# Head sums in an RWKV7 mixer: from float32 products to pairs of float32r products, with two prefetch windows moved

## The chip, the cores and the metric

The kernel is one launch on 1 core of a Trainium2 chip. The metric is the time of that launch on the device in microseconds; the median of several runs is quoted, and every row shown comes from one further run that was profiled.

## The reference, cut to what matters

A diffusion transformer of four layers runs over 256 latent and 256 context tokens with 1024 features. Layers 0 and 3 mix tokens by grouped attention, layer 1 by neighbourhood attention, and layer 2 by a bidirectional RWKV7 recurrence; each is followed by a squared-ReLU MLP. The change touches layer 2 alone. There are 16 heads of 64 features, and the sums over a head's 64 features are these:

```python
kk = (k * p['k_k']).reshape(hs)
kk = kk * lax.rsqrt(jnp.maximum(jnp.sum(kk * kk, -1, keepdims=True), 1e-12))
...
mu = jnp.mean(y, -1, keepdims=True)
var = jnp.mean(jnp.square(y - mu), -1, keepdims=True)
y = (y - mu) * lax.rsqrt(var + RW_GN_EPS) * lnx_g + lnx_b
bonus = jnp.sum(jnp.sum(r[None] * k_dir * p['r_k'], -1, keepdims=True), axis=0) * v
y = (y + bonus).reshape(g.shape)
return (y * g) @ p['wo']
```

`y` is the sum of a forward and a backward scan with the state update `s = s*w + (s a) b + v k`. Between these sums lie the projections r, k, v (1024 x 1024 each), three low-rank gates and the scan.

## The kernel before

**Engines.** PE multiplies, ACT casts, copies and evaluates functions, DVE does tensor arithmetic, POOL solves small triangular systems, and SP issues all the DMAs named here.

**Weight products.** A large product is made of float32r products. `split` (L423 to L425) turns a float32 tile into a high part, a cast on ACT, and a low part, a subtraction on DVE; weights are split alike at L280 after their load into `wr`. `mm3` (L430 to L432) then issues three products for each block of 128 features: high by high, high by low, low by high. The projections r and k go through `gemm` (tile `mm`), v through `values` (tile `vps`, L479 to L481).

**The mixer.** `rwkv` works on pairs of heads: pair c holds 128 rows (two heads of 64) and 512 columns (tokens, in 8 blocks of 64), so there are 8 pairs. A sum over a head's 64 rows is a product with `ones64`, a 128 x 128 matrix with two blocks of ones, in plain float32. For each pair there are four lists of steps:

- `prep(c)`, 13 steps: the gates (`gate_products`: products into `wps`, then functions on ACT into `sg` and `ag`), `unit_k` (Square into `ksq`, head sum `kss` at L1192, then Ln and Exp), decays by a scan, `triangles` (product `tps`, masked by DVE into `TT`, the backward one transposed into `dc`, stored to DRAM as `dr`), and `solve` (DMA `dr` into `lane`, POOL solves, DMA to `rr`, DMA into `S`).
- `inverses(c)`, 10 steps: DVE transposes `S` into `R` (L1313), the products `pa`, `pb`, `pv`, `px` and the copies `Xt<-M` and `Xt<-px` put together the inverse of each 64 x 64 triangle.
- `core(c)`: the scan over 8 blocks in two directions; for each block products `nps`, `zps`, copy `z`, product `ups`, copy `u`, then `yps` and the state `sps`.
- `post(c)`, 6 steps: `mean` (copy `y` out of PSUM, sum `gm`, centring on DVE at L1486, Square into `ysq`), `bonus` (sum `bo`, transposed v into `vT`), `var` (sum `gv`, Ln, Exp), `normed`, `gated` (product `g` of 128 x 128 by 128 x 512) and `parts` (the split of `o`, the operand of the last projection).

**What sets the order.** Every step carries a due time counted in pairs; all steps are sorted by it and written out in that order, so each engine works through one fixed list. `over(steps, a, b)` spreads steps evenly from a to b:

```python
todo = over([keys(c) for c in range(8)], -2.6, -1.5)
todo += over([values(j, t) for j in range(4) for t in TOKS], -1.35, .3)
for c in range(8):
    main = core(c)
    todo += [(c + x / len(main), f) for x, f in enumerate(main)]
    todo += over(inverses(c), c - .65, c - .1)
    todo += over(post(c), c + 1, c + 1.6) if c < 7 else []
```

So prep runs one and a half to two and a half pairs ahead, and the stretch ahead of the first core, here called the transition, holds the key projections, the prep of pairs 0 and 1, and the value projections. The last `post` is woven with the beginning of the output projection (`mm<-o`). Tiles come from pools: `ps_s` gives the PSUM banks of the head sums, `tmp` and `pair` those in SBUF.

Of the kernel before, what the change touches and what calls it, by code (L numbers as in the profile page):

```python
# [10 lines left out]
F32 = mybir.dt.float32  # L11
F32R = mybir.dt.float32r
# [181 lines left out]
def dit_kernel(ctx: ExitStack, tc: tile.TileContext, places, t_in, out, layers=DEPTH):  # L194
# [767 lines left out]
    def rwkv(i, hx, gate, nrm, begun, ends):  # L962
# [36 lines left out]


        xx = [pair("xx") for _ in range(4)]

# [159 lines left out]
        def prep(c):  # L1162
# [24 lines left out]

            def unit_k():
                sq = tmp(512, "ksq")
                act.activation(out=sq, in_=k_, func=AF.Square, scale=C("k_k", "rw")[:, c:c + 1])  # L1190
                ps = bank(ps_s, 512, "kss")
                pe.matmul(ps, lhsT=ones64, rhs=sq, start=True, stop=True)  # L1192
                dve.tensor_scalar(out=sq, in0=ps, scalar1=1e-12, scalar2=None, op0=ALU.max)
                log(out=sq, in_=sq, func=AF.Ln)
                log(out=sq, in_=sq, func=AF.Exp, scale=-0.5)
                q["nkk"] = tmp(512, "nkk")
                dve.scalar_tensor_tensor(out=q["nkk"], in0=k_, scalar=nkk_c[:, c:c + 1], in1=sq, op0=ALU.mult, op1=ALU.mult)
# [279 lines left out]
        def post(c):  # L1477
            q = st[c]
            hold = {}

            def mean():
                y = tmp(512, "y")
                act.copy(out=y, in_=q["y"])
                ps = bank(ps_s, 512, "gm")
                pe.matmul(ps, lhsT=ones64, rhs=y, start=True, stop=True)
                dve.scalar_tensor_tensor(out=y, in0=ps, scalar=-1.0 / 64, in1=y, op0=ALU.mult, op1=ALU.add)  # L1486
                sq = tmp(512, "ysq")
                act.activation(out=sq, in_=y, func=AF.Square)
                hold["y"], hold["sq"] = y, sq

            def bonus():
                ps = bank(ps_s, 512, "bo")
                pe.matmul(ps, lhsT=ones64, rhs=q["rkd"], start=True, stop=True)
                bo = q["rkd"]
                act.copy(out=bo, in_=ps)
                pt = bank(ps_s, 512, "vT")
# [3 lines left out]
                dve.tensor_tensor(out=bo, in0=pt, in1=bo, op=ALU.mult)  # L1500
                hold["bo"] = bo

            def var():
                ps = bank(ps_s, 512, "gv")
                pe.matmul(ps, lhsT=ones64, rhs=hold["sq"], start=True, stop=True)
                r = hold["sq"]
                log(out=r, in_=ps, func=AF.Ln, bias=epg, scale=1.0 / 64)
                log(out=r, in_=r, func=AF.Exp, scale=-0.5)
# [6 lines left out]
            def gated():  # L1515
                ps = bank(ps_s, 512, "g")
                g2 = sml.tile([128, 128], F32, tag="g2", bufs=1, name="g2")
                sp.dma_start(out=g2, in_=t_in["rws"][c, :, 2])
                pe.matmul(ps, lhsT=g2, rhs=sig, start=True, stop=True)
                y = hold["y"]  # L1520
                dve.tensor_tensor(out=y, in0=y, in1=hold["bo"], op=ALU.add)
                dve.tensor_tensor(out=y, in0=y, in1=ps, op=ALU.mult)

            def parts():
                o[c] = pair("o", F32R)
                split(o[c], hold["y"], 0, 512)
            return [mean, bonus, var, normed, gated, parts]

# [34 lines left out]
        for c in range(8):  # L1563
            main = core(c)
            todo += [(c + x / len(main), f) for x, f in enumerate(main)]
            todo += over(inverses(c), c - .65, c - .1)
            todo += over(post(c), c + 1, c + 1.6) if c < 7 else []
            if c >= RHELD:
                todo.append((c - 2.9, lambda c=c: fetch(c)))
        for c in range(8):  # L1570
# [3 lines left out]
            def step(k, c=c, made_=made_):  # L1574
# [4 lines left out]
                return go  # L1579
            todo += over([step(k) for k in range(9)], c - 2.4, c - 1.5)  # L1580
            todo += over([step(k) for k in range(9, 13)], c - 1.4, c - .9)
        todo.append((7., last_weights))
# [216 lines left out]
```

## Time and profile before

| | us |
|---|---|
| median of 3 runs | 2552.61 |
| lowest and highest | 2551.04, 2557.27 |
| the profiled execution | 2547.62 |
| its span, first to last instruction | 2545.2 |
| PE busy in the span | 2448.7 (96%) |
| DVE busy | 1664.0 (65%) |
| ACT busy | 1188.7 (47%) |
| POOL busy | 209.2 (8%) |
| mean granted clock of PE | 0.987 |

The mixer's stretch lies between about 1240 and 1830 us of the span: gates, keys and values up to about 1440, the eight pairs from there to about 1800, and then the last `post`. A group's row names a line of the kernel, an engine, an operation and its tiles; its numbers are the busy time of the group, the mean of one in ns and, behind the bar, the idle time of the engine ahead of it. A float32 product of 128 x 512 leaves two records in the trace, so sixteen records are eight products.

### The profile page before, as it was taken

What the parts mean: (1) busy time and instruction counts of PE and PEld (TensorE: products, weight loads), DVE (VectorE), ACT (ScalarE), POOL (GpSimd) and SP (SyncE); (2) the same over time, 40 slices, a digit from 0 to 9 for tenths busy, and PEclk for the clock granted to TensorE, in tenths of its full rate; (3) what the DMA queues carried; (4) which work ended last, traced back from release to release, by engine and by line L of the source; (5) the groups of instructions that cost most, each with busy time, mean ns of one, the idle gap of its engine ahead of it and who ended that gap; (6) DMA issues with size and microseconds to landing.
All of it is one profiled execution on the core that took longest, in us unless ns stands there. A gap on an engine that the chain in (4) does not pass through costs nothing. (4 is left out here: it accounts for less than half of the span.)

```text
span 2545.2 us, 53184 instructions
## 1 busy us (share of the span) xinstructions
PE 2448.7 (96%) x22337; PEld 2085.8 (82%) x22337; DVE 1664.0 (65%) x3087; ACT 1188.7 (47%) x2226; POOL 209.2 (8%) x383
## 2 busy tenths in 40 slices
PE   8999999999999999999889799899999999998998
PEld 5779888889766988888867677778898888998997
DVE  4567777775566777787786565673567663766555
ACT  3555443244566543334555444544362343465644
POOL 0002000002000110000202112211020000121000
PEclk9999999999999999999999999999999999999999
DMA  8432556642211245665132311210336654223553
GB/s 337 166 127 75 182 189 192 207 157 88 69 55 58 88 152 182 207 205 176 60 112 77 80 28 33 41 20 15 143 107 216 206 184 126 93 68 115 175 184 98
DMA packets 158415, 324.11 MB, mean 127 GB/s; under 512 B 77393, under 2 KB 80993, under 8 KB 158177
## 3 DMA queue, kind: packets, MB, share of 16 engines
q1 hardware_dynamic: 158176, 320.73, 39.8%
q8 instruction: 175, 2.87, 0.5%
q14 instruction: 64, 0.52, 0.1%
HBM read 310.71 MB, written 9.97 MB: 126 GB/s over the span
## 5 line engine op out<-in xcount | busy, mean ns | idle before, releaser
L430 PE MATMUL mm<-h,wh 128*128 128x512 f32 (+1 forms) x1472 | 515.5, 351 | 6.1 <-ACT h L180 4.7
L432 PE MATMUL mm<-h,wl 128*128 128x512 f32 (+1 forms) x1472 | 511.6, 348 | 1.1 <-DVE wl L280 1.1
L280 DVE TENSOR_TENSOR wl<-wr,wh 128x1024 fp32r<-128x1024 f32 x363 | 442.7, 1227 | 103.5 <-ACT wh L180 77.9
L431 PE MATMUL mm<-h,wh 128*128 128x512 f32 (+1 forms) x1472 | 510.0, 347 | 0.3 <-DVE h L425 0.2
L180 ACT CAST wh<-wr 128x1024 fp32r<-128x1024 f32 x363 | 373.8, 1049 | 261.7 <-DVE wl L280 89.2
L430 PE MATMUL mm<-f,wh 128*128 128x512 f32 (+1 forms) x1168 | 397.6, 340 | 0.0
L432 PE MATMUL mm<-f,wl 128*128 128x512 f32 (+1 forms) x1168 | 397.6, 340 | 0.0
L431 PE MATMUL mm<-f,wh 128*128 128x512 f32 (+1 forms) x1168 | 397.0, 340 | 0.0
L430 PEld LDWEIGHTS mm<-h,wh 128*128 128x128 f32 x1472 | 279.4, 190 | 50.0 <-issue 8.8
L432 PEld LDWEIGHTS mm<-h,wl 128*128 128x128 f32 x1472 | 279.8, 190 | 37.1 <-issue 3.0
L431 PEld LDWEIGHTS mm<-h,wh 128*128 128x128 f32 x1472 | 279.8, 190 | 34.5 <-issue 2.8
L431 PEld LDWEIGHTS mm<-f,wh 128*128 128x128 f32 x1168 | 221.6, 190 | 24.7
L430 PEld LDWEIGHTS mm<-f,wh 128*128 128x128 f32 x1168 | 221.6, 190 | 24.5
L432 PEld LDWEIGHTS mm<-f,wl 128*128 128x128 f32 x1168 | 221.6, 190 | 24.2
L180 ACT ACTIVATE relu<-mm 128x512 f32<-128x512 f32 (+1 forms) x146 | 72.5, 497 | 360.4 <-PE mm L432 360.3
L425 DVE TENSOR_TENSOR f<-sqr,f 128x512 fp32r<-128x512 f32 (+1 forms) x146 | 82.4, 567 | 210.4 <-ACT f L180 210.4
L492 DVE SCALAR_TENSOR_TENSOR x<-mm,gate,x 128x256 f32<-128x256 f32 x280 | 127.3, 480 | 128.5 <-PE mm L432 128.3
L544 POOL TENSOR_SCALAR x<-zc,cs 128x256 f32<-128x256 f32 x88 | 86.0, 990 | 1302.9 <-DVE zc L575 1302.9
L387 DVE SCALAR_TENSOR_TENSOR mwt<-mwt,srow 128x1024 f32<-128x1024 f32 x144 | 175.8, 1221 | 8.3 <-DMA mwt<-in_mwr_dram 6.9
L387 DVE SCALAR_TENSOR_TENSOR mpr<-mwt,srow 128x1024 f32<-128x1024 f32 x112 | 136.7, 1220 | 0.5
L430 PE MATMUL mm<-o,wh 128*128 128x256 f32 (+1 forms) x400 | 120.1, 302 | 0.3 <-ACT o L180 0.2
L432 PE MATMUL mm<-o,wl 128*128 128x256 f32 (+1 forms) x400 | 119.9, 300 | 0.1
(292 smaller groups left out, 4317.9 us busy)
## 6 DMA issues: line engine op xcount, KB each, us to landing
wr<-in_gw_dram SPq DMA_DIRECT2D x363, 512.0 KB, 3.7
mwt<-in_mwr_dram SPq DMA_DIRECT2D x144, 512.0 KB, 4.3
mwt<-in_mw_dram SPq DMA_DIRECT2D x48, 512.0 KB, 5.4
srow<-srow_d SPq DMA_DIRECT2D x6, 512.0 KB, 4.1
nab<-in_nab_dram SPq DMA_DIRECT2D x8, 384.0 KB, 3.3
rk<-rk_d SPq DMA_DIRECT2D x6, 512.0 KB, 5.1
rk_d<-rkp SPq DMA_DIRECT2D x10, 256.0 KB, 2.2
x<-in_xt_dram SPq DMA_DIRECT2D x4, 512.0 KB, 10.2
```

The costliest lines, as they stand in the source:

```text
L180: x = f(*args, **kw)
L280: self.lo[self.done % len(self.lo)].tensor_tensor(out=lo, in0=t, in1=hi.bitcast(F32), op=ALU.subtract)
L387: dve.scalar_tensor_tensor(out=to, in0=t, scalar=1.0, in1=rw_["s"][cnd], op0=ALU.mult, op1=ALU.mult, accum_out=m[:, cnd, r * 8 + c:r * 8 + ...
L425: eng.tensor_tensor(out=dst[:, 1, a:b], in0=src, in1=dst[:, 0, a:b].bitcast(F32), op=ALU.subtract)
L430: pe.matmul(ps, lhsT=st, rhs=hl[:, 0, a:b], start=first, stop=False)
L431: pe.matmul(ps, lhsT=st, rhs=hl[:, 1, a:b], start=False, stop=False)
L432: pe.matmul(ps, lhsT=wl[:, c * 128:(c + 1) * 128], rhs=hl[:, 0, a:b], start=False, stop=last)
L492: dve.scalar_tensor_tensor(out=xc(c)[:, a:b], in0=ps[:, a - base:b - base], scalar=gate[:, cnd, c:c + 1], in1=xc(c)[:, a:b], op0=ALU.mult, ...
L544: (eng or dve).tensor_scalar(out=dst, in0=src, scalar1=ca, scalar2=cb, op0=ALU.mult, op1=ALU.add)
```

## The change

It has three parts, all in `rwkv`.

1. The four float32 head sums of a pair become two float32r products each. `in_parts` casts the operand to a high part on ACT and subtracts on DVE for the low part; `over_heads` multiplies both by `sums64`, the float32r copy of `ones64`. For the mean, the matrix is `less64` (identity minus `ones64`/64), so that `gm` comes out centred and the centring on DVE goes. y is no longer copied before `gm`; its parts are cast from PSUM, and the centred y is copied from `gm`. `unit_k` is cut in two steps, so `prep` has 14; `post` has 8. The product `g` moves from `gated` to `var`, the load of its weights to `bonus`.
2. `inverses(c)` goes in two groups: six steps from c - .74 to c - .42, four from c - .28 to c - .06.
3. The first ten steps of pair 0's `prep` go from -2.55 to -1.9 (nine from -2.4 to -1.5 before); those of other pairs keep their window.

```diff
@@ -998,6 +998,21 @@
         dve.tensor_scalar(out=ka1, in0=C("k_a", "rw"), scalar1=-1.0, scalar2=1.0, op0=ALU.mult, op1=ALU.add)
 
 
+        sums64 = sml.tile([128, 128], F32R, tag="sums64", bufs=1, name="sums64")
+        act.copy(out=sums64, in_=ones64)
+        less64 = sml.tile([128, 128], F32R, tag="less64", bufs=1, name="less64")
+        dve.scalar_tensor_tensor(out=less64, in0=ones64, scalar=-1.0 / 64, in1=ident, op0=ALU.mult, op1=ALU.add)
+
+        def in_parts(src):
+            t = pair("ip", F32R)
+            split(t, src, 0, 512)
+            return t
+
+        def over_heads(ps, w, parts):
+            for x in (1, 0):
+                pe.matmul(ps, lhsT=w, rhs=parts[:, x], start=x == 1, stop=x == 0)
+
+
         xx = [pair("xx") for _ in range(4)]
 
 
@@ -1185,11 +1200,16 @@
                 sigmoids(todo)
             out.append(gate_products)
 
-            def unit_k():
+            def square_k():
                 sq = tmp(512, "ksq")
                 act.activation(out=sq, in_=k_, func=AF.Square, scale=C("k_k", "rw")[:, c:c + 1])
+                q["ksq"] = in_parts(sq)
+            out.append(square_k)
+
+            def unit_k():
                 ps = bank(ps_s, 512, "kss")
-                pe.matmul(ps, lhsT=ones64, rhs=sq, start=True, stop=True)
+                over_heads(ps, sums64, q.pop("ksq"))
+                sq = tmp(512, "ksr")
                 dve.tensor_scalar(out=sq, in0=ps, scalar1=1e-12, scalar2=None, op0=ALU.max)
                 log(out=sq, in_=sq, func=AF.Ln)
                 log(out=sq, in_=sq, func=AF.Exp, scale=-0.5)
@@ -1478,31 +1498,37 @@
             q = st[c]
             hold = {}
 
-            def mean():
-                y = tmp(512, "y")
-                act.copy(out=y, in_=q["y"])
-                ps = bank(ps_s, 512, "gm")
-                pe.matmul(ps, lhsT=ones64, rhs=y, start=True, stop=True)
-                dve.scalar_tensor_tensor(out=y, in0=ps, scalar=-1.0 / 64, in1=y, op0=ALU.mult, op1=ALU.add)
-                sq = tmp(512, "ysq")
-                act.activation(out=sq, in_=y, func=AF.Square)
+            def taken():
+                hold["yp"], hold["bp"] = in_parts(q["y"]), in_parts(q["rkd"])
+
+            def centred():
+                po, ps = bank(ps_s, 512, "bo"), bank(ps_s, 512, "gm")
+                over_heads(po, sums64, hold.pop("bp"))
+                over_heads(ps, less64, hold.pop("yp"))
+                y, sq = tmp(512, "y"), tmp(512, "ysq")
+                act.activation(out=sq, in_=ps, func=AF.Square)
+                act.copy(out=y, in_=ps)
+                act.copy(out=q["rkd"], in_=po)
                 hold["y"], hold["sq"] = y, sq
 
+            def squares():
+                hold["sp"] = in_parts(hold["sq"])
+
             def bonus():
-                ps = bank(ps_s, 512, "bo")
-                pe.matmul(ps, lhsT=ones64, rhs=q["rkd"], start=True, stop=True)
                 bo = q["rkd"]
-                act.copy(out=bo, in_=ps)
                 pt = bank(ps_s, 512, "vT")
                 for blk in range(8):
                     for e in range(2):
                         pe.matmul(pt[half[e], blk * 64:blk * 64 + 64], lhsT=V[blk // 2][half[e], blk % 2, c], rhs=ident[half[e], half[e]], start=True, stop=True)
                 dve.tensor_tensor(out=bo, in0=pt, in1=bo, op=ALU.mult)
                 hold["bo"] = bo
+                hold["g2"] = sml.tile([128, 128], F32, tag="g2", bufs=1, name="g2")
+                sp.dma_start(out=hold["g2"], in_=t_in["rws"][c, :, 2])
 
             def var():
-                ps = bank(ps_s, 512, "gv")
-                pe.matmul(ps, lhsT=ones64, rhs=hold["sq"], start=True, stop=True)
+                ps, hold["g"] = bank(ps_s, 512, "gv"), bank(ps_s, 512, "g")
+                over_heads(ps, sums64, hold.pop("sp"))
+                pe.matmul(hold["g"], lhsT=hold["g2"], rhs=sig, start=True, stop=True)
                 r = hold["sq"]
                 log(out=r, in_=ps, func=AF.Ln, bias=epg, scale=1.0 / 64)
                 log(out=r, in_=r, func=AF.Exp, scale=-0.5)
@@ -1513,18 +1539,14 @@
                 affine(y, y, C("lnx_g", "rw")[:, c:c + 1], C("lnx_b", "rw")[:, c:c + 1])
 
             def gated():
-                ps = bank(ps_s, 512, "g")
-                g2 = sml.tile([128, 128], F32, tag="g2", bufs=1, name="g2")
-                sp.dma_start(out=g2, in_=t_in["rws"][c, :, 2])
-                pe.matmul(ps, lhsT=g2, rhs=sig, start=True, stop=True)
-                y = hold["y"]
+                y, ps = hold["y"], hold["g"]
                 dve.tensor_tensor(out=y, in0=y, in1=hold["bo"], op=ALU.add)
                 dve.tensor_tensor(out=y, in0=y, in1=ps, op=ALU.mult)
 
             def parts():
                 o[c] = pair("o", F32R)
                 split(o[c], hold["y"], 0, 512)
-            return [mean, bonus, var, normed, gated, parts]
+            return [taken, centred, squares, bonus, var, normed, gated, parts]
 
         resets = tmp(520, "resets")
         dve.memset(resets, 1.0)
@@ -1563,7 +1585,8 @@
         for c in range(8):
             main = core(c)
             todo += [(c + x / len(main), f) for x, f in enumerate(main)]
-            todo += over(inverses(c), c - .65, c - .1)
+            inv = inverses(c)
+            todo += over(inv[:6], c - .74, c - .42) + over(inv[6:], c - .28, c - .06)
             todo += over(post(c), c + 1, c + 1.6) if c < 7 else []
             if c >= RHELD:
                 todo.append((c - 2.9, lambda c=c: fetch(c)))
@@ -1577,8 +1600,8 @@
                         made_.extend(prep(c))
                     made_[k]()
                 return go
-            todo += over([step(k) for k in range(9)], c - 2.4, c - 1.5)
-            todo += over([step(k) for k in range(9, 13)], c - 1.4, c - .9)
+            todo += over([step(k) for k in range(10)], *((c - 2.4, c - 1.5) if c else (-2.55, -1.9)))
+            todo += over([step(k) for k in range(10, 14)], c - 1.4, c - .9)
         todo.append((7., last_weights))
         for _, f in sorted(todo, key=lambda p: p[0]):
             f()
```

The instructions of the layers outside `rwkv` and all of POOL stand in the same order in both kernels. Three places of the order follow; behind the line number stands the instruction, its output and operands, and a count.

PE in the transition, before: `kss` of pair 0, its two `tps` batches, `kss` of pair 1, then the first `pa`. Between them lie products of keys (`mm`) and of values (`vps`).

```order
L1192 MATMUL kss<-ksq,cs_rw 128x512
...
L1263 MATMUL tps<-AR,BK 64x64 x16
...
L1263 MATMUL tps<-AR,BK 64x64 x16
...
L1177 MATMUL wps<-lora,wa 128x512 x4
...
L1192 MATMUL kss<-ksq,cs_rw 128x512
...
L1322 MATMUL pa<-R,TT 32x32 x17
```

PE in the transition, of the change:

```order
L1013 MATMUL kss<-ip,sums_11521 128x512 x2
...
L1283 MATMUL tps<-AR,BK 64x64 x32
...
L1192 MATMUL wps<-lora,wa 128x512 x3
...
L1013 MATMUL kss<-ip,sums_11521 128x512 x2
...
L1342 MATMUL pa<-R,TT 32x32 x32
L1342 MATMUL pa<-S,TT 32x32 x32
```

Counted on PE's list, the first `kss` (row 6250) and the first `pa` (row 6516) stand where they stood; the two `tps` batches move from rows 6347 and 6372 to row 6300, and the second `kss` moves from row 6440 to row 6490.

DVE up to the first `R<-S`, before:

```order
L1193 TENSOR_SCALAR ksq<-kss 128x512
L280 TENSOR_TENSOR wl<-wr,wh 128x1024 x2
L1197 SCALAR_TENSOR_TENSOR nkk<-rk,nkk_c,ksq 128x512
L1206 TENSOR_TENSOR cc<-sg 128x520 x2
L1142 COPY rV<-vps 64x128 x2
L1313 STREAM_TRANSPOSE R<-S 128x512
```

DVE up to the first `R<-S`, of the change:

```order
L425 TENSOR_TENSOR ip<-ksq,ip 128x512
L1213 TENSOR_SCALAR ksr<-kss 128x512
L1157 COPY rV<-vps 64x128 x2
L1217 SCALAR_TENSOR_TENSOR nkk<-rk,nkk_c,ksr 128x512
L1157 COPY rV<-vps 64x128 x2
L1226 TENSOR_TENSOR cc<-sg 128x520 x2
L1333 STREAM_TRANSPOSE R<-S 128x512
```

In both, pair 1's unit-key work stands ahead of pair 0's `R`; with `kss` fifty rows later on PE, it stands closer to it.

ACT in the loop, where pair 0's `post` (ops on `y`, `ysq`, `bo`) meets the `prep` of a later pair (`sg`, `cc`, `ag`) and the block copies `z` and `u`, before:

```order
L180 ACTIVATE sg<-cc 128x520
L180 COPY Xt<-px_16305 32x8x32
L180 ACTIVATE cc<-cc 128x520
L180 COPY z<-zps 128x128
L180 ACTIVATE sg<-cc 128x520
L180 COPY bkt<-bkt 128x256
L180 COPY u<-ups 128x128
L180 ACTIVATE cc<-cc 128x520
L180 COPY z<-zps 128x128
L180 ACTIVATE ag<-ag,ka_11519,cs_rw 128x512
L180 COPY y<-yps 128x512
```

The same place on ACT, of the change:

```order
L180 CAST ip<-yps 128x512
L180 ACTIVATE cc<-cc 128x520
L180 CAST ip<-ag 128x512
L180 ACTIVATE sg<-cc 128x520
L180 COPY z<-zps 128x128
L180 ACTIVATE cc<-cc 128x520
L180 COPY u<-ups 128x128
L180 COPY bkt<-bkt 128x256
L180 COPY ag<-bo 128x512
L180 ACTIVATE ysq<-gm 128x512
L180 COPY y<-gm 128x512
L180 CAST ip<-ysq 128x512
```

Casts of the parts of y and of the bonus now stand ahead of a block's `z`, and four operations on the results stand ahead of the next block's `z`, which follows this piece.

## Rows read from the trace of the kernel before

**Rows 1.** Page, busy time by engine: us, share, count.

```profile
PE 2448.7 (96%) x22337; PEld 2085.8 (82%) x22337; DVE 1664.0 (65%) x3087; ACT 1188.7 (47%) x2226; POOL 209.2 (8%) x383
```

**Rows 2.** Windows: us, busy PE, PEld, DVE, ACT, POOL, granted clock, DMA share, GB/s.

```profile
1340.00:1400.00 60.00, 54.51 (x322) 44.76 (x321) 38.64 (x58) 29.97 (x44) 16.21 (x34) 0.94 0.29 82
1400.00:1500.00 100.00, 82.57 (x1745) 73.43 (x1745) 55.70 (x118) 40.13 (x89) 21.11 (x62) 0.93 0.25 56
1500.00:1700.00 200.00, 182.19 (x5114) 147.71 (x5112) 124.89 (x263) 105.24 (x236) 42.52 (x131) 0.97 0.20 35
1700.00:1830.00 130.00, 125.43 (x3209) 105.41 (x3206) 67.50 (x137) 53.91 (x127) 8.30 (x30) 1.00 0.24 76
```

**Rows 3.** Waits of PE, 1400 to 1500: us in total, times, longest.

```profile
PE vps L479 <- ACT wh L180: 4.9, 2, 3.5
PE pa L1322 <- DVE R L1313: 3.9, 1, 3.9
PE nps L1392 <- ACT rV L180: 2.5, 1, 2.5
PE pv L1357 <- DVE xd L1344: 1.2, 1, 1.2
```

**Rows 4.** Waits of PE, 1500 to 1700.

```profile
PE kss L1192 <- ACT ksq L180: 6.9, 5, 1.5
PE ups L1426 <- ACT z L180: 2.7, 5, 0.7
```

**Rows 5.** Timeline of PE, `gm` of two pairs that follow each other: start, us, instruction.

```profile
1512.95 1.12 PE L1485 MATMUL gm<-y,cs_rw 128*128 128x512 f32 x2
...
1560.31 1.12 PE L1485 MATMUL gm<-y,cs_rw 128*128 128x512 f32 x2
```

**Rows 6.** Timeline of PE in the last post.

```profile
1810.99 0.39 PE L432 MATMUL mm<-o,wl 128*128 128x512 f32 x1
1811.21 1.02 PE L1485 MATMUL gm<-y,cs_rw 128*128 128x512 f32 x2
1812.07 1.02 PE L1493 MATMUL bo<-ag,cs_rw 128*128 128x512 f32 x2
1813.02 1.15 PE L1499 MATMUL vT<-cs,rV 64*64 64x64 f32 x32
1814.20 1.13 PE L1505 MATMUL gv<-ysq,cs_rw 128*128 128x512 f32 x2
```

**Rows 7.** Groups by line, 1240 to 1900: busy, mean ns | idle before.

```profile
L1486 DVE SCALAR_TENSOR_TENSOR y<-gm,y 128x512 f32<-128x512 f32 x8 | 5.5, 692 | 9.8 <-PE gm L1485 9.6
L180 ACT ACTIVATE ysq<-y 128x512 f32<-128x512 f32 x8 | 5.1, 633 | 5.7 <-DVE y L1486 5.7
L180 ACT COPY y<-yps 128x512 f32<-128x512 f32 x8 | 4.8, 595 | 2.3 <-PE yps L1462 2.3
```

**Rows 8.** Timeline of ACT, then PE, where a later pair's prep meets the loop.

```profile
1592.58 2.50 ACT L180 COPY Xt<-M 32x512 f32<-32x512 f32 x4
1595.10 0.72 ACT L180 ACTIVATE ksq<-rk,cs_rw 128x512 f32<-128x512 f32 x1
1595.88 1.13 PE L1192 MATMUL kss<-ksq,cs_rw 128*128 128x512 f32 x2 [1.45 <-ACT ksq L180]
```

**Rows 9.** Timeline of the transition: start, us, engine (SPq is SP's DMA issue).

```profile
1371.39 2.52 SPq L1272 DMA_DIRECT2D dr<-dc  x4
1398.30 1.77 SPq L1295 DMA_DIRECT2D rr<-lane  x2
1402.46 1.54 SPq L270 DMA_DIRECT2D wr<-in_gw_dram  x2
1405.36 0.71 DVE L1313 STREAM_TRANSPOSE R<-S 128x512 f32<-128x512 f32 x1 [7.96 <-DMA S<-rr]
1406.13 0.74 PE L1322 MATMUL pa<-R,TT 32*32 32x32 f32 x34 [3.91 <-DVE R L1313]
1410.37 0.58 PE L479 MATMUL vps<-wh,mh 128*128 128x256 f32 x1 [3.50 <-ACT wh L180]
```

## The prediction

> **What bounds the kernel now.** I read the busy times first. PE is busy 96% of the span, DVE 65%, ACT 47% [rows 1]: PE is the engine whose time counts, and only its work and its waits can change the end. The change touches one mixer, so the windows of that stretch come next [rows 2]. They show four regimes. From 1340 to 1500, the transition ahead of the pairs and the first pair, PE is idle 5.5 + 17.4 us and its granted clock is 0.94 and 0.93, that is, a part of the stretch runs at the lower of the two levels (1.2 instead of 2.4 GHz). From 1500 to 1700, the loop in which each pair also prepares a later one, PE is idle 17.8 of 200 us, ACT busy 53% and DVE 62%. From 1700 on no prep is left, PE is idle 4.6 of 130 us. So waits are to be had mainly before 1500, PE work everywhere.
>
> What the waits are is read next. In the transition PE waits for `R` (3.9 us), for a weight cast (4.9), for v's copies (2.5) and for `xd` (1.2), 12.5 us in all [rows 3]. In the loop its largest wait is `kss` for the Square `ksq`: 6.9 us in 200, five times, up to 1.5 [rows 4]. From one `gm` to the next a pair takes 47.4 us there [rows 5], so 200 us hold 4.2 pairs and the wait is 1.6 us a pair. The waits for `z` are small, 2.7 us. I take these, not ACT's busy share, as the measure of what ACT costs now.
>
> **The sums as pairs of float32r products.** A float32r product of 128 x 512 starts 0.22 to 0.23 us after the one before it; `gm` takes 0.86 us until `bo` starts and `bo` 0.95 until `vT` starts [rows 6]. Two float32r products are 0.46, so a sum gives back 0.40 to 0.49 us of PE; I take 0.45. Four sums a pair: 1.8 us; 8 pairs: 14.4 us of PE's work.
>
> Against that stand four casts more on ACT in each pair (four of `in_parts` and the copy of y from `gm`, less the copy from `yps`) at 0.595 us, the copy of that shape [rows 7]: 2.4 us. DVE gains four subtractions and loses the centring, which costs 0.692 [rows 7]; I cost a subtraction of that shape the same, so 2.1 us a pair. In the loop's rates ACT goes from 24.7 to 27.1 us in a pair of 47, DVE from 29.3 to 31.4 [rows 2]. Neither becomes the bound by its sum. What counts is the place: ACT takes its list in order. In the change the casts of y and of the bonus parts stand ahead of a block's `z`, and the copy of `bo`, the Square, the copy of y and a cast ahead of the next block's `z`, while y's copy stood behind it. PE's `ups` waits for `z`. Each of the two blocks gets one to two operations of 0.6 us ahead of a `z` that was already waited for [rows 4], 1.2 to 2.4 us a pair. I take 1.7, the middle; the other blocks' `z` stay as they are.
>
> In the last post the chain from `yps` to the end of the head sums has a subtraction and two casts more, 0.69 + 1.2 us, but the centring goes (0.69), and the change puts output-projection products between `gm` and `gv`: two and nine of them, 2.5 us by 0.227 each, and `vT`, 1.2 [rows 6], where now PE goes straight from `vT` to `gv`. The chain there (Square 0.63, two copies, a cast, a subtraction, about 3.1 [rows 7]) is covered by 3.7. So I cost the tail at its saved products alone. Without that cover it would cost the 3.1 us once.
>
> **Inverses in two groups, and the Square.** Now four copies `Xt<-M`, 2.50 us, stand right ahead of `ksq` on ACT, and `kss` waits 1.45 for it [rows 8]. With the first group of `inverses` from c - .74, these copies leave that burst: in the change they stand between the `z` copies ahead of the table loads, where PE has the gates' products. `ksq` itself is a step earlier than `kss` now. Its cast and subtraction add 0.6 + 0.69 us to its own chain; the room is the 2.50 us that left. I take back 1.0 of the 1.6 us a pair; the bounds are 0 (the wait changes its name to the cast, or to the scan that follows on DVE) and 1.6.
>
> **The transition.** Today `dr<-dc` is issued at 1371.39 and `R` runs at 1405.36 [rows 9]: 34.0 us for storing the triangles, POOL's solve until `rr` at 1398.30, and the way back. The change puts both `tps` batches 47 and 72 rows of PE earlier, at 0.227 us a row 11 and 16 us. With `dc` behind both, `dr<-dc` comes at about 1356, and `S` lands at about 1390. SP keeps three loads of `wr` ahead of the way back; they wait for products that lie some 70 rows (16 us) behind the new `tps`, before POOL has ended by the new times (1398.30 less 15), so I cost them at nothing; were they late, `S` would come later by as much, with 11 us of room before it mattered.
>
> PE then comes to `pa` with nothing to wait for in `S`. But the order shows what is late next: on DVE `R` stands behind pair 1's unit-key work, and `kss` for that is now 26 rows ahead of `pa` instead of 76. At half the columns and so about half of 0.227 us a row PE passes it at about 1398 to 1399; behind it come the maximum, Ln, Exp, `nkk` and two products `cc`, six operations of 0.63 to 0.69 us, 4.1 us, and `R`, 0.71. So `pa` starts at about 1403 instead of 1406.1: 3 us of the 3.9. The loads of `wr` for v, issued at 1402.46 behind `S` [rows 9], come some 12 us earlier; the wait for their cast, 3.5 us behind `pa`, has no reason left but the queue of copies on ACT: I take back 2. With `Xt<-M` and `pv` earlier in the order, of the waits for v's copies and `xd` (2.5 + 1.2) another 2; and of the clock, whose lost part in 1400 to 1500 is 7% of 100 us, 1. Together 8 us. The least is 3 (`pa` alone), the most 12, which is all four waits of rows 3.
>
> Part 3 alone reaches only pair 0, so it is in this sum and in no other.
>
> **The sum.** The six pairs whose prep runs in the loop: -1.8 + 1.7 - 1.0 = -1.1 us each, -6.6 (bounds +0.6 and -2.2 each: +3.6 to -13). The two pairs with no prep left beside them, three sums each and little on ACT: -1.2 each, -2.4 (0 to -2.7). The transition: -8 (-3 to -12). In all -17 us: 2547.6 - 17.0 = 2530.6 for an execution like the profiled one. The median of the runs shown lies 5.0 above the profiled time, so I forecast 2535.6, 0.7% faster. All bounds at once give +0.6 and -27.7.
>
> **The rivals.**
>
> *Slower: the casts queue up behind one another.* Place: ACT and DVE between the last `yps` of a pair and its `gv`. If every added operation is served serially while PE waits, a pair costs 2.4 + 2.1 = 4.5 us more against 1.8 less: +2.7 for six pairs, +16.2; the transition at its least, -3; the last pairs nothing. That is 2547.6 + 13.2 + 5.0 = 2566. It decides the sign from 3.5 us of new waits a pair on, twice what I take (the 1.8 saved, and 8 + 2.4 of the rest divided by six, with nothing back at `kss`). For it: the four operations ahead of each of the two `z` in the order, DVE at 62%, and waits for `z` already there. Against it: those waits come to 0.6 us a pair now, with functions and copies ahead of many a `z` already. The Trainium skill ("TensorE: Matmul & The Clock Gate", the specification table) calls the queues of ScalarE and VectorE strict FIFOs, while TensorE can pull weight loads ahead; by that rule the casts can't be passed, and this rival would be exact, where independent copies could slip by its price would fall to nothing. The trace agrees so far as it has `z` behind whatever stands ahead of it; no run here shows yet how much of it PE feels.
>
> *No change: the transition keeps its end.* If `R` waits for pair 1's unit-key work until 1406, PE stays where it is, and the pairs' savings go into the new waits. Then -3 from the transition's cast and 0 to -3 from the pairs: 2547 to 2550. For it: the second `kss` is 50 rows later on PE. Against it: `wr` comes 12 us earlier in any case.
>
> *All of it counts.* PE is the most used engine, so its 14.4 us and the waits for `R`, the cast and `kss` come back in full and the casts hide: -14.4 - 9.6 - 12 = -36, 2517. For it: ACT at 53% in the loop has room by sum. Against it: `kss` and `ups` wait for ACT at that share already [rows 4]. The Trainium skill ("Perfetto Trace Analysis", "Identifying the Most-Contended Engine") would have the engine with the highest occupancy optimized first; that speaks for this rival. The loop's waits for ACT, an engine at half load, differ from it, and the measured rows decide for me.
>
> **How the numbers follow.** A change of 0.3% (7.7 us) is about what a measurement of this kernel can tell from none. Forecast case, 8 to 26 us less: 0.53. All counts: 0.07. No change, 0 to 8 us less, or slightly more: 0.26. Slower by the queue: 0.14. Hence faster 0.60, same 0.26, slower 0.14. For 8 in 10 the range takes the forecast case and most of no change: from 2522 (2535.6 less the 10.7 to the lower bound, and 2.9 for the clock, of which 0.93 leaves more to come back than I took) up to 2554 (the upper bound of +0.6 on 2552.6, rounded up).
>
> **What would show it.** In the trace of the change `gm` should follow `bo` after about 0.46 us; `dr<-dc` should be issued near 1356 and `S` land near 1390; `pa` should start near 1403, and the first pair's work behind it about 7 us earlier than now. In the loop the wait of `kss` should be at most 0.6 us a pair, the waits for `z` 2 to 2.5. The distance from one `gm` to the next, 47.4 us now, should fall by about 1, and by 1 to 1.5 in the last two pairs. I am wrong if `S` lands after 1400, if PE waits for `z` or for parts over 3.5 us a pair, or if these distances grow.

## The result and the profile after

The change takes 2525.09 us (median of 4, 2524.59 to 2526.62) against 2551.82 for the kernel before, measured beside it (four runs, 2548.69 to 2557.27): a ratio of 0.9896 (95% interval 0.988 to 0.9913), 1.0% or 26.7 us faster. The profiled execution of the change took 2526.62 us with a span of 2524.8. The forecast was 2535.6, with a range from 2522 to 2554: right in sign and inside the range, about 10 us short.

The windows of the mixer's stretch in the change answer to [rows 2]; the columns are the same (busy us of PE, PEld, DVE, ACT and POOL, then granted clock, DMA share and GB/s).

```profile
1340.00:1400.00 60.00, 54.20 (x343) 45.62 (x344) 38.99 (x64) 29.67 (x48) 10.59 (x32) 0.91 0.44 121
1400.00:1500.00 100.00, 90.30 (x2019) 80.41 (x2012) 62.12 (x128) 51.40 (x112) 21.78 (x62) 0.95 0.21 42
1500.00:1700.00 200.00, 183.47 (x5502) 154.67 (x5500) 144.21 (x303) 115.12 (x250) 44.22 (x130) 0.99 0.18 31
1700.00:1830.00 130.00, 123.71 (x2709) 111.84 (x2706) 67.77 (x137) 53.83 (x122) 9.32 (x31) 1.00 0.25 77
```

PE's idle time between 1400 and 1500 falls from 17.4 to 9.7 us. In the loop ACT's load rises from 53% to 58% and DVE's from 62% to 72%, and PE is idle hardly less (16.5 for 17.8), but at a clock of 0.99 for 0.97.

Where the 20.4 us between the two spans went is read by marks that both traces have, the first `zps` (before, then in the change) and the starts of `gm` (in the change; before in [rows 5]):

```profile
1455.32 0.45 PE L1414 MATMUL zps<-rV,nmo 64*64 64x64 f32 x8
...
1445.52 0.40 PE L1434 MATMUL zps<-rV,nmo 64*64 64x64 f32 x8
...
1499.90 0.63 PE L1013 MATMUL gm<-ip,less 128*128 128x512 f32 x2
...
1544.72 0.63 PE L1013 MATMUL gm<-ip,less 128*128 128x512 f32 x2
```

The first `zps` comes 9.8 us earlier, the first `gm` 13.1 us. From there the next four `gm` follow at 44.8, 45.8, 44.8 and 45.3 us, for 47.4, 45.9, 48.8 and 47.5: another 8.8 us. The last three distances, 40.2, 36.4 and 32.8 for 38.8, 34.7 and 35.2, give 0.6 back, and all behind the last `gm` 0.9. So 13 us lie ahead of the first head sum of `post`, 9 in the four pairs with a prep beside them, and the rest gives 1.5 back.

PE's waits in the loop of the change, 1500 to 1700 (in all, times, longest), answer to [rows 4]:

```profile
PE ups L1446 <- ACT z L180: 3.1, 8, 0.6
PE yps L1477 <- DVE ip L425: 2.9, 4, 0.7
...
PE zps L1438 <- DVE s L1467: 2.3, 4, 0.6
PE nps L1412 <- DVE nmo L1415: 2.2, 4, 0.5
```

The wait of `kss` for `ksq`, 6.9 us before, is gone. The wait for `z` is about what it was (2.7 us before). New is a wait of `yps` for the subtraction that makes the low part of the last pair's y: `yps` has one bank, and it is free only when both parts have been read.

The transition of the change, PE, DVE and SP's issues out of the timeline, answers to [rows 9]:

```profile
1352.63 1.78 SPq L1292 DMA_DIRECT2D dr<-dc  x4
...
1373.36 1.33 SPq L1315 DMA_DIRECT2D rr<-lane  x2
1376.73 0.38 SPq L1317 DMA_DIRECT2D S<-rr  x1
...
1380.11 1.11 SPq L270 DMA_DIRECT2D wr<-in_gw_dram  x2
...
1394.48 0.69 DVE L1213 TENSOR_SCALAR ksr<-kss 128x512 f32<-128x512 f32 x1 [0.82 <-PE kss L1013]
...
1397.85 1.31 DVE L1226 TENSOR_TENSOR cc<-sg 128x520 f32<-128x520 f32 x2
1399.08 0.70 DVE L1333 STREAM_TRANSPOSE R<-S 128x512 f32<-128x512 f32 x1
...
1399.84 0.72 PE L1342 MATMUL pa<-R,TT 32*32 32x32 f32 x62 [2.40 <-DVE R L1333]
...
1401.87 0.58 PE L479 MATMUL vps<-wh,mh 128*128 128x256 f32 x1 [0.72 <-ACT wh L180]
```

`S` is issued at 1376.73 and lands 3.3 us later, 19 us before `R` runs. `R` has no idle time ahead of it on DVE: it stands behind `nkk` and `cc` of pair 1, and PE still waits 2.40 us. The weights' cast keeps PE 0.72 us for 3.50.

And PE in the last post of the change, as in [rows 6]:

```profile
1789.51 0.63 PE L1013 MATMUL bo<-ip,sums 128*128 128x512 f32 x2
1789.98 0.63 PE L1013 MATMUL gm<-ip,less 128*128 128x512 f32 x2
1790.44 0.39 PE L430 MATMUL mm<-o,wh 128*128 128x512 f32 x1
...
1793.80 0.62 PE L1013 MATMUL gv<-ip,sums 128*128 128x512 f32 x2
```

A sum takes 0.46 to 0.47 us for 0.86 to 0.95, and `gv` follows behind its eleven products without a wait.

### The profile page after: what moved, and what is told of

Read it like the earlier page. It is cut to its first block, busy times and chain, and to the rows that moved or that the text cites. A ratio compares the mean times of both kernels' runs of the same rounds, so it can differ in the third digit from the quotient of the medians.

```text
span 2524.8 us, 53255 instructions
## 1 busy us (share of the span) xinstructions
PE 2434.9 (96%) x22337; PEld 2086.8 (83%) x22337; DVE 1675.3 (66%) x3112; ACT 1207.0 (48%) x2259; POOL 206.7 (8%) x383
## 4 chain that ended last, share of the span: by engine, by line
PE 88%; DVE 5%; ACT 5%; issue 2%; DMA 1%; SPq 0%; ACTq 0%; DVEq 0%
PE mm L430 22%; PE mm L432 21%; PE mm L431 21%; PE ptp L652 2%; PE op L801 1%; PE op L921 1%; PE vps L479 1%; PE vps L481 1%; PE mdp L322 1%; PE vps L480 1%; PE ups L1446 1%; PE bkt L1424 1%; PE nps L1414 1%; DMA mwt<-in_mw_dram 1%; PE sc L890 1%
## 5 line engine op out<-in xcount | busy, mean ns | idle before, releaser
L432 PEld LDWEIGHTS mm<-h,wl 128*128 128x128 f32 x1472 | 280.6, 191 | 37.4 <-issue 3.0
L431 PEld LDWEIGHTS mm<-h,wh 128*128 128x128 f32 x1472 | 280.6, 191 | 34.2 <-issue 2.8
```

Source lines behind the costliest of these rows:

```text
L431: pe.matmul(ps, lhsT=st, rhs=hl[:, 1, a:b], start=False, stop=False)
L432: pe.matmul(ps, lhsT=wl[:, c * 128:(c + 1) * 128], rhs=hl[:, 0, a:b], start=False, stop=last)
```

## The experiments

All differences below are medians against the kernel before, measured beside them in the same one of three groups of runs (e1 to e4: 2548.8 us, e5 to e8: 2551.1, e9 to e12: 2550.7). The interval of such a difference reaches some 3 to 5 us to either side. Where a text says "lost to the clock", it counts half of the time at a granted clock of 0.50, which is what the time costs if PE has work throughout. Three parts make eight combinations, and all were run.

**Part 1 alone (e1).** The edit is the change without these two pieces:

```diff
-            inv = inverses(c)
-            todo += over(inv[:6], c - .74, c - .42) + over(inv[6:], c - .28, c - .06)
+            todo += over(inverses(c), c - .65, c - .1)
...
-            todo += over([step(k) for k in range(10)], *((c - 2.4, c - 1.5) if c else (-2.55, -1.9)))
+            todo += over([step(k) for k in range(10)], c - 2.4, c - 1.5)
```

> Part 1 alone: the head sums as float32r products, with the inverses and the prep of pair 0 in their old windows. My theory (a pair saves 1.8 us of PE, the casts ahead of z take 1.7 of it back where a prep runs beside, the wait of kss stays, since Xt<-M stays ahead of ksq): 6 pairs at -0.1, the last two at -1.2, and nothing in the transition: -3 us, between -7 and +4 against before. Rival 'all of PE's time comes back': -14 us. Rival 'the casts queue': +8 us or more.

Measured: 2561.45, 12.7 us slower (ratio 1.0049, 1.0036 to 1.0062). My theory fell: a pair takes 51 to 52 us from `gm` to `gm`, not 47 (in the profiled execution, the slowest of five with 2568.1 us). The rival in which the casts queue named the sign and the size, 8 us or more.

**Part 2 alone (e2)**, the first of the two pieces above put into the kernel before.

> Part 2 alone: the inverses in two groups, the sums in float32. My theory: the copies Xt<-M leave the burst ahead of ksq, the wait of kss (1.6 us a pair) goes: -1.6 x 6 = -10 at most, -6 as taken; in the transition xd and the copies come earlier, -2: -8 us in all. Rival 'the burst is bound by something else' (the wait takes another name): within 2 us of before.

Measured: 2540.93, 7.9 us faster (0.9966, 0.9955 to 0.9978), as expected. Only the first loop pair's `kss` still waits for `ksq` (0.39 us); the others have no wait. The grouping takes more away than that: no `ups` between the first and the fifth `gm` waits over 0.15 us for `z`, and a pair takes 44.0 to 46.2 us. But the last three distances, 40.8, 37.1 and 36.4, are 5.5 us longer together than before.

**Part 3 alone (e3)**, in the kernel before:

```diff
-            todo += over([step(k) for k in range(9)], c - 2.4, c - 1.5)
+            todo += over([step(k) for k in range(9)], *((c - 2.4, c - 1.5) if c else (-2.55, -1.9)))
```

> Part 3 alone: pair 0's prep earlier. My theory: R waits for pair 1's unit-key work instead of S, 3 us at pa, and the weights of v come earlier, 2 us: -5 us, within -2 and -8. Rival 'the transition keeps its end': within 2 us. Rival 'S was all that held it': -8 us or more, with pa no longer waiting for R.

Measured: 2535.55, 13.2 us faster (0.9947, 0.9935 to 0.9958); the third answer. Without the new casts and with `kss` of pair 1 where it stood, `R` is done before PE comes to `pa`. The timeline of DVE, then PE, in e3:

```profile
1396.51 0.71 DVE L1313 STREAM_TRANSPOSE R<-S 128x512 f32<-128x512 f32 x1
...
1401.31 0.49 PE L1322 MATMUL pa<-R,TT 32*32 32x32 f32 x34
```

`pa` waits for nothing there; in the change it waits 2.40 us.

**Parts 2 and 3 (e4).**

> Parts 2 and 3 without part 1. My theory, by which the three parts add up: -8 and -5, -13 us against before; the rest of the change's -27 would then have to be part 1's, -14, which is PE's full saving. If instead the parts need each other (grouping only pays with the cheap sums), this is -5 us or less, and part 1 is worth 20 on top.

Measured: 2527.34, 21.4 us faster (0.9915, 0.9903 to 0.9927). The two windows add up, 7.9 and 13.2, and give most of the change by themselves. On top of them part 1 is worth 3 to 5 us, by the change's 24.7 to 26.7. Where that comes from, the marks show, e4's against those of the change and of the same kernel again (e7): the first `gm` comes at 1496.0 for 1499.9 and 1500.4, the next four distances make 182.4 us for 180.7 and 179.8, the last three 113.3 for 109.4 and 108.3. So part 1 costs 4 us ahead of the first `gm`, gives about half a us in a pair with a prep, and 4 to 5 us in the last three distances.

**Parts 1 and 3 (e5).**

> The change without part 2 (sums and pair 0's earlier prep, inverses in their old window). Theory now, after the sums alone cost 12.5 us: it is the old window of the inverses that makes the sums dear, since the copies Xt<-M and v stand in ACT's burst together with the new casts, so PE waits for z and v and its clock falls. Then this is the prep's -13.5 plus the sums' +12.5: between -4 and +3 us against before, with 51 to 52 us from one gm to the next. Rival 'the sums were dear in the transition only' (the first ten steps of pair 0's prep): -13 or better.

Measured: 2559.93, 8.8 us slower (1.0036, 1.0024 to 1.0048), with 51.1 to 52.7 us a pair. That is above the -4 to +3 that I expected. So the sums cost 22 us beside the earlier prep alone, and it is the old window of the inverses that makes them dear. Its ACT shows why, at two places. The first is the timeline from the second table load to the copies `v`:

```profile
1595.71 1.28 ACT L180 ACT_TABLE_LOAD   x1
1597.00 2.50 ACT L180 COPY Xt<-M 32x512 f32<-32x512 f32 x4
1599.52 0.72 ACT L180 ACTIVATE ksq<-rk,cs_rw 128x512 f32<-128x512 f32 x1
1600.15 0.24 ACT L180 COPY v<-pv 128x128 f32<-128x128 f32 x1
1600.30 0.62 ACT L180 CAST ip<-ksq 128x512 fp32r<-128x512 f32 x1
```

and PE at the same place:

```profile
1600.45 0.45 PE L1434 MATMUL zps<-rV,nmo 64*64 64x64 f32 x8 [1.99 <-ACT v L180]
...
1601.41 0.44 PE L1424 MATMUL bkt<-cs,BK 64*64 64x64 f32 x6 [0.28 <-ACT bkt L180]
...
1601.97 1.22 PE L1013 MATMUL kss<-ip,sums 128*128 128x512 f32 x2
```

ACT is one unbroken list of work from the second table load on, the first `v` stands behind 4.4 us of it, and PE waits 1.99 us for that copy. In the change the four copies `Xt<-M` stand elsewhere, and `ksq` follows the table load at once:

```profile
1577.18 1.28 ACT L180 ACT_TABLE_LOAD   x1
1578.47 0.72 ACT L180 ACTIVATE ksq<-rk,cs_rw 128x512 f32<-128x512 f32 x1
1579.10 0.24 ACT L180 COPY v<-pv 128x128 f32<-128x128 f32 x1
```

The second place is where the casts of y and of the bonus come into a row of functions ahead of a `z`, here on ACT one pair earlier:

```profile
1558.70 1.17 ACT L180 ACTIVATE sg<-cc 128x520 f32<-128x520 f32 x2
1559.77 0.62 ACT L180 ACTIVATE cc<-cc 128x520 f32<-128x520 f32 x1
1560.30 0.57 ACT L180 CAST ip<-yps 128x512 fp32r<-128x512 f32 x1
1560.76 0.63 ACT L180 CAST ip<-ag 128x512 fp32r<-128x512 f32 x1
1561.28 0.64 ACT L180 ACTIVATE cc<-cc 128x520 f32<-128x520 f32 x1
1561.82 0.26 ACT L180 COPY z<-zps 128x128 f32<-128x128 f32 x1
```

PE's two largest waits between 1500 and 1700 are these two, and neither is in e3 at this size (there `z` 2.4 us, 0.5 at most, and `v` none, but `kss` for `ksq` 5.7):

```profile
PE ups L1446 <- ACT z L180: 8.6, 8, 1.6
PE zps L1434 <- ACT v L180: 6.0, 3, 2.0
```

The waits are half of it. From the first `gm` to the fifth a pair takes 5.1 us more than in e3; PE is idle 3.3 us more and busy 1.8 us more, although the products give 1.8 back. That difference, 3.6, goes to the clock, whose falls there have 4.3 us a pair lost. Windows of 4 us of e5 around the first place, columns as above:

```profile
1594.00:1598.00 4.00, 3.01 (x112) 2.25 (x112) 2.80 (x5) 3.54 (x5) 3.37 (x9) 1.00 0.00 0
1598.00:1602.00 4.00, 1.74 (x55) 1.30 (x41) 0.71 (x2) 3.47 (x9) 0.57 (x3) 0.97 0.30 37
1602.00:1606.00 4.00, 4.00 (x65) 3.17 (x66) 0.79 (x2) 1.92 (x5) 0.00 (x0) 0.50 0.70 111
1606.00:1610.00 4.00, 4.00 (x102) 3.67 (x98) 2.92 (x6) 1.67 (x7) 0.44 (x2) 0.68 0.32 122
```

PE is busy 4.75 of 8 us, and then its granted clock is 0.50, the lower of the two levels, for some 6 us. In e5 that happens at this burst five times between 1499 and 1715, once a pair and for 6.8 to 10.2 us; that adds up to some 20 us lost to the clock between 1500 and 1840, and in e1 to 24. In the profile of the kernel before it happens twice, behind `kss`'s wait (5 us), in those of e2, e3 and e4 not at all.

**Parts 1 and 2 (e6).**

> The change without part 3 (sums and grouped inverses, pair 0's prep in the old window). Theory now: with the grouping the sums cost nothing in the loop, a pair takes 45 to 46 us as without them, and the transition keeps its old place: -8 to -13 us against before. Rival 'the sums need pair 0's earlier prep': 0 or slower.

Measured: 2532.52, 18.6 us faster (0.9926, 0.9914 to 0.9938): better than expected, 10.7 us better than part 2 alone. `pa` waits 5.4 us for `R` in it, and a pair takes 44.8 to 45.5 us, on average 45.2 as in e2. So none of the 10.7 us lies in the pairs with a prep: the first `gm` comes 6.4 us earlier than in e2, and the last three distances are 3.9 us shorter. Why part 1 helps ahead of the first `gm` here and costs 4 us there beside part 3 is open.

**The change again (e7).**

> The change as it is, beside the others of this call for a direct comparison: -24 to -27 us against before. A clock that falls at other places in its profile than in the first one would show that the places are not set by the order.

Measured: 2526.49, 24.7 us faster (0.9907, 0.9893 to 0.9922). The dips of the clock in the transition come at the same places (near 1380, 1400 and 1435); one near 1680 in the first profile is absent here.

**Each pair of products twice (e8).**

```diff
-            for x in (1, 0):
+            for x in (1, 0, 1, 0):
```

> The change with each pair of products of a head sum issued twice (the second overwrites the first), so that PE spends on a sum what the float32 product took, and ACT and DVE do what they do in the change: the worth of the cheaper product by itself. Forecast's theory: the waits behind the sums take part of it up, +5 to +11 us on the change. Rival 'PE's time counts in full': 8 x 4 x 0.46 = +14.7 us. Rival 'the products lie in waits anyway': within 2 us of the change.

Measured: 2538.04, 13.1 us faster than before (0.9948, 0.9935 to 0.996), so 11.5 us slower than e7. The intervals leave room for 7 to 16. In the trace `gm` follows `gm` after 46.3 to 47.3 us for 44.8 to 45.2, 1.8 us a pair on average: that is the full 1.84 of the four products. The rival, PE's time in full, fits the trace best; my 5 to 11 was too low for the pairs.

**Ten idle products a pair in e5 (e9).**

```diff
+        def fill(k):
+            ps = bank(ps_s, 512, "fill")
+            for x in range(k):
+                pe.matmul(ps, lhsT=sums64, rhs=some, start=True, stop=True)
...
                     act.copy(out=hold["v1"][:, g0:g0 + 4], in_=pv)
+                    if g0 and c:
+                        fill(10)
```

> The kernel of e5 (sums and pair 0's earlier prep, old window of the inverses) with ten idle float32r products, 2.3 us of PE, added to each later pair's inverses, where PE waits for xd and v; their output is not used. In e5 PE's granted clock falls to the lower level for some 6 us behind that wait in five pairs of five, which costs 3 us each time; the waits themselves are about 3 us. Theory now, that half of what the sums cost without the grouping is the clock: with PE kept at work there the clock stays, and the kernel is 10 to 18 us faster than e5 in spite of 16 us more work for PE, near 2545. Rival 'the waits alone cost it': the added products lie in waits at best, the same as e5, 2558 to 2562, or slower by up to 16 us.

Measured: 2554.34, 3.6 us slower than before (1.0016, 1.0006 to 1.0027) where e5 was 8.8 slower (1.0036): 5 us faster than e5, with some 1 to 9 us by the intervals, and with 16 us more work for PE. The window of 1500 to 1700, first of e5:

```profile
1500.00:1700.00 200.00, 172.76 (x4799) 145.48 (x4800) 126.11 (x261) 101.21 (x222) 40.60 (x123) 0.92 0.17 32
```

and of e9:

```profile
1500.00:1700.00 200.00, 180.96 (x5009) 149.29 (x5005) 130.30 (x273) 109.98 (x243) 42.38 (x130) 0.99 0.18 32
```

The granted clock goes from 0.92 to 0.99. From the first `gm` to the fifth e9 needs 195.6 us for 206.8, 2.8 us a pair less; the next two distances, where there was less wait to fill, grow from 40.1 and 34.2 to 43.9 and 37.4. The wait for `v` is gone, since PE now spends it on the filler, and the wait for `z` is still there (8.1 us for 8.6). So the clock is shown as a cause, worth some 3 us a pair beyond what the filler cost; my total was too high because I left out the pairs that pay for it.

**The old window for the last pair (e10).**

```diff
-            todo += over(inv[:6], c - .74, c - .42) + over(inv[6:], c - .28, c - .06)
+            todo += (over(inv[:6], c - .74, c - .42) + over(inv[6:], c - .28, c - .06) if c < 7 else over(inv, c - .65, c - .1))
```

> The change with the old window for the inverses of the last pair alone. From the gm of pair 5 to that of pair 6, the distance grew from 34.7 us to 36.4 with the grouping, and with the sums alone it was 34.5: where no prep runs beside, there is no burst to leave. Theory: 2 us faster than the change, about -28 us against before. Rival 'it was the sums': no difference.

Measured: 2525.72, 25.0 us faster than before (0.9911, 0.9893 to 0.9929): the same as the change, and the distance in question stays at 36.6. The theory fell. The rival, that it was the sums, has this result for it, but e2 and e4 against it: the distance is 36.0 to 37.6 us in every kernel with part 2, with float32 sums (37.1 in e2 and e4) as with the new ones, and 34.2 to 35.2 without part 2 (37.4 in e9, with its filler). So it comes with the grouping, but not by the last pair's own window; by what is open.

**As e10, with ten idle products ahead of the first `pa` (e11).**

```diff
                 def go():
+                    if c == 0 and d == 0:
+                        fill(10)
                     pa = bank(ps_s, 256, "pa").rearrange("p (g t) -> p g t", g=8)
```

> As e10, and ten idle products on PE right ahead of the first pa, which waits 2.4 us for R; behind that wait the clock is at the lower level for about 7 us, 3.5 us lost. Theory of the clock: another 2 to 4 us faster, about -31 us against before. Rival 'other waits near it pull the clock down anyway': the same as e10.

Measured: 2524.05, 26.7 us faster than before (0.9896, 0.988 to 0.9913), 1.7 below e10. In the trace the wait for `R` is gone, the time lost to the clock between 1340 and 1500 falls from 8.5 to 5.1 us and the first `gm` comes 3.1 us earlier, at 1497.9; the total is not separable from e10 or from the change.

**Each cast twice (e12).**

```diff
             t = pair("ip", F32R)
+            act.copy(out=t[:, 0], in_=src)
             split(t, src, 0, 512)
```

> The change with each cast of in_parts made twice on ACT (the same values to the same place): 32 casts of 0.6 us more on ACT, 19 us, and the parts come 0.6 us later. The forecast's theory has one to two operations of 0.6 us ahead of a z that is waited for in two blocks of a pair: +0.6 to +1.2 us each, for six to eight pairs +4 to +10 us. Rival 'ACT at half load has room': within 2 us of the change. Rival 'everything behind the casts is served serially': +19 us.

Measured: 2539.06, 11.7 us faster than before (0.9955, 0.994 to 0.9971), so 12 to 13 us slower than the change and above the 4 to 10 of my theory. PE's waits between 1500 and 1700 show the place:

```profile
PE yps L1478 <- DVE ip L425: 9.8, 5, 2.0
PE ups L1447 <- ACT z L180: 4.6, 9, 0.8
```

The wait of `yps` for y's parts goes from 0.7 to 2.0 us each; the wait for `z` hardly moves. `gm` follows `gm` after 47.6 to 48.4 us for 44.8 to 45.2, 3 us more for 2.4 us of casts. The waits are half of these 3 us: PE is idle 5.6 us in a pair for 4.0 in e7. The other half is the clock again: behind that wait of `yps` it falls to 0.50 four times between 1500 and 1651, for 3.4 to 6.8 us, and in e7 not once. My theory left that out.

The eight combinations in one table, us against before (an entry of the last column is uncertain by some 5 us):

| | without part 1 | with part 1 | part 1 adds |
|---|---|---|---|
| neither window | 0 | +12.7 | +12.7 |
| part 3 | -13.2 | +8.8 | +22 |
| part 2 | -7.9 | -18.6 | -10.7 |
| parts 2 and 3 | -21.4 | -24.7 to -26.7 | -3 to -5 |

Part 1 is more than cheaper products and casts: it spreads fourteen steps of prep over the window of thirteen, and moves `g`. No run separates these two from the rest; e8 and e12 test the products and the casts by themselves.

## Why the prediction was right, and where it was off

The forecast was 10.5 us short, and by two things. The execution profiled was forecast at 2530.6 us and took 2526.6, 4 us less. The other 6.5 us are the step from a profile to the median: I added the 5.0 us by which the median of before lay above its profile, but the change's median lies 1.5 us below its own (last paragraph of this section).

**The products.** Costed at 0.45 us saved a sum, 1.8 a pair; a sum now takes 0.46 for 0.86 to 0.95, and by e8's marks a pair pays the 1.84 in full. Right.

**The casts.** I had 1.7 us a pair of new waits, all of them for `z`. Against e4, which has both windows and the old sums, PE is idle 4.0 to 4.1 us a pair for 2.6, so the casts bring 1.4 (1.7 by e2 and e6). The size was right, the place half right: the grouping takes the waits for `z` away, as e2 and e4 show, and the casts bring 0.8 us of them back, so that against before nothing seems to have changed; another 0.7 lies at the single bank of `yps`, and 0.5 at `nps`, which waits for `nmo` from DVE; some small waits of e4 are gone in return. Without the grouping (e5) `z` is waited for 2.1 us a pair, which is the 2 to 2.5 that I named as the sign. With -1.8 and +1.4 to +1.7 part 1 gives next to nothing in a pair with a prep, as my terms said. That part 1 on top of both windows measured -3 to -5, where they add up to -4.2 (8 x -1.8 and 6 x 1.7), is in part luck: by e4's marks part 1 costs 4 us ahead of the first `gm`, where these terms have nothing of the kind, and gives somewhat more than they have behind it.

**The Square's burst.** I took back 1.0 of the 1.6 us a pair that `kss` waited. All of it went, and with it the falls of the clock behind that wait, which my sum priced only in the transition. I had 1.1 us for each of six pairs: four gained 2.2 each and pair 0's own blocks, from the first `zps` to the first `gm`, 3.3, while the sixth has no Square beside it (the last `kss` lies ahead of the fifth `gm`) and lost 1.4. In all -10.7 for -6.6; within the stretch that is the term that was mis-sized. e2, with part 2 alone, has the same 2.2 us in the four pairs.

**The transition.** Forecast -8 up to the first blocks, measured -9.8 at the first `zps` (-8.5 in e7). `dr<-dc` was forecast for 1356 and came at 1352.6; `S` was forecast to land at 1390 and landed at 1380, because the way from `dc` to `S` took 27.4 us, not 34.0 as before; 5 of these 6.6 us lie between the issue of `lane` and that of `rr`, where POOL solves, and why it needs less there is open. That error cost nothing, for the reason the forecast named: `R` stands behind pair 1's unit-key work, and `pa` started at 1399.8 (1401.6 in e7; forecast 1403) with 2.4 us of wait left. e3 shows the other side of it: without the sums `R` is not late and part 3 is worth 13.2 us; with the sums and the grouping 6 to 8. Beside e4, where `pa` waits for nothing and 3.4 us are lost to the clock between 1340 and 1500, the change has that wait and 8.5 to 10.2 us lost. Of SP's three `wr` loads ahead of the way back, which I costed at nothing, none is late: the last is issued by 1366.8, before `rr`.

**The last pairs and the tail.** Forecast -2.4 for the two, measured -0.8 by the last two distances; the last three together gave 0.6 back, and two of the three grew, which I had named as a sign of being wrong. The products were saved (e8's distances are 0.9 to 1.5 us longer there), but part 2 costs more than that: against the same kernel without it, e2, e4, e6, the change and e7 are 1.4 to 5.5 us longer in the three distances, by a cause that e10 didn't find. In the tail `gv` doesn't wait, as costed; the saving itself, at most 2 us, can't be seen there, since the time behind the last `gm` differs by 2.4 us between kernels with the same tail (732.5 in e5, 734.9 in the change).

**The slower rival.** Its place and its point of decision were right, and it is what happens to part 1 without part 2: +4 to +5 us a pair in e1 and e5 against before. Its price of 2.7 lacked the clock: behind the longer wait PE runs at the lower level for some 6 us, and that costs about as much as the waits. I had put the grouping down as a gain of 1.0 us a pair beside the sums, where it is what makes the sums pay: with the sums, part 2 is worth 31 to 34 us, without them 8. The Trainium skill ("TensorE: Matmul & The Clock Gate", the specification table) has ACT as a strict FIFO: the trace agrees, `v` and `z` come out behind whatever stands ahead of them. The rule of the Trainium skill ("Perfetto Trace Analysis", "Identifying the Most-Contended Engine") to work on the engine with the highest occupancy first is not enough for part 1 by itself: it takes 14 us from the engine with 96% and the kernel gets 12.7 us slower.

**From the profile to the median.** The spans of the two profiles differ by 20.4 us, the medians by 24.7 to 26.7. The runs of before scatter (2544 to 2557 us in 43), those of the change hardly (2524.6 to 2530.3 in eight). What goes with it is the mean granted clock of each run, in the 39 runs of before beside the experiments. At 0.989 and 0.990 they take 2544.1 to 2544.5 us, at 0.987 2547.1 to 2550.7, at 0.985 2551.2 to 2553.6, at 0.983 2555.4 and 2555.9; the change's eight runs have 0.987 or 0.988. So the profiled execution of before (0.987) is one with less lost to the clock than its median run, and part of what the medians differ by is that the change's clock scatters less. Where in these runs the clock falls is not shown; in the profile it is the transition, the waits of `kss`, and places outside the mixer.

## What to carry to other kernels

A cheaper product on the busiest engine pays only if the work that prepares its operands doesn't land where that engine already waits for the preparing one: look for the burst on that other engine first, move what can move out of it, then spend there. When a wait on PE grows, price it twice: the wait, and the clock behind it, read from the granted clock just after similar waits in the same trace. A wait that looks unchanged can be one that one edit took away and another brought back. And test edits of one change in all combinations: here two of them added up, and the third changed sign with its company.

## What was not expected of the hardware

In e5 a row of waits, none over 2.0 us and 3.25 us together within 8 us in the place shown, was followed by some 6 us at a granted clock of 0.50; the same place in the pair has such a fall in five pairs in a row. Ten idle products in that place held the clock at 0.99 over the loop, and a kernel with 16 us more work for PE ran 5 us faster.
